# Reordering the output stage of a hybrid decoder layer: recurrent products earlier, transposes later, loads in another order

## The chip, the core and the metric

The kernel runs on one core of a Trainium2 chip. Its engines work side by side, each through its own queue in order: TensorE (PE: matrix products and transposes), VectorE (DVE), ScalarE (ACT), GpSimd (POOL), and SyncE (SP), from whose queue all loads and stores of this stage are issued. They wait for each other through semaphores. PE writes its results to PSUM, here in banks of 128 x 512 float32; the other data lie in SBUF. The metric is the device time of one execution in microseconds (us).

## The reference

One layer of a Hymba-like decoder: 1024 tokens and 16 meta tokens, width 1024, float32. Two groups of heads (a gated delta rule, "GDN", and a forgetting attention, "FoX") share one input projection and one output projection; then comes a SwiGLU block.

```python
u = rmsnorm(h, attn_norm_w[l])
proj = u @ w_in[l]
...
o_gdn = gated_deltanet_group(...)
o_fox = forgetting_attention_group(fq, fk, fv, ff, fgate_b[l]).astype(h.dtype)
h = h + jnp.concatenate([o_gdn, o_fox], axis=-1) @ w_out[l]
h = h + swiglu(rmsnorm(h, ffn_norm_w[l]), w_gate[l], w_up[l], w_down[l])
...
h = rmsnorm(h, final_norm_w)
return h[:, N_META:]
```

The change lies in the next to last product: the output projection, the residual add, the norm ahead of the SwiGLU block, and the transposes that this block needs.

## The kernel before

**Products.** A float32 product is made of three products of parts: each operand is split into a high part (ACT casts, L160) and the rest (DVE subtracts, L161). `mm3` issues high x high (L190), high x low weight (L191), low x high (L192), so the third product of a group is the first that needs the low part of the data. Products are 128 x 128 by 128 x 512; four k-tiles make a group of 12.

**The output stage.** The 1024 rows are 8 tiles of 128, worked in `ORDER` = 0, 4, 1, 5, 2, 6, 3, 7. Below, name(t) is the step of tile t. The left 512 columns of a tile's result are half 0, the right 512 half 1. The steps of a tile:

- `prep_load`: `of` is loaded (512 KB, two attention parts of 128 x 512 each), POOL adds the two parts (L1114), ACT copies the reciprocal row sums into the free half (L1115). There are two `of` buffers.
- `prep_pe`: PE transposes the sums (4 transposes, `rbt`, L1125), DVE multiplies (L1126), ACT and DVE split the result into `ohl`.
- `load_h`: the residual `hst` is loaded (512 KB; for the tiles of `fused` its halves come from `x` and from `h_d`, 256 KB each). There are two `hst` buffers.
- `fox_g`: for the tiles of `fused` (4, 5, 2, 6, 3, 7) the 12 products of the GDN heads for half 1 (`wx<-whi_wo,uh_p`). They depend on nothing of this stage. They are the recurrent products of the title. Their bank (tag "mm", one buffer) is held until `hst` of this tile takes half 1.
- `out_fox(t, 0)`: 12 products (`wof`) and DVE's add to `hst` (L1158). `out_fox(t, 1)`: 12 products (`wx<-wf,ohl` into the bank of `fox_g`, or `wof<-wf`) and the add; then the norm: ACT squares (L1051), DVE scales (`st_f`, L205), POOL takes the power (`st_f`, L206), DVE multiplies by `nwb`, the norm's weights (`xn`, L1053). The tile is stored to `h_d`.
- `u_blocks`: 8 transposes of `xn` into two banks (`u2t`, L1229; tag "tp", three buffers) and their evictions: for tiles 0 to 3 casts and copies on ACT and two subtractions `ul_p` on DVE (L1235); for tiles 4 to 7 also sums for the 7-product scheme of the SwiGLU block, on DVE (`br`, `ub`, `ut`, `ul_p`), ACT and POOL (`br`, L1254, and two `ul_p`).

In step i of the loop (L1402) PE's order is as written: `out_fox(t, 0)`, `prep_pe` of the next tile, `fox_g(t)`, `u_blocks` of the tile before, `out_fox(t, 1)`; for i = 1 and 2 `u_blocks` comes last. What stands ahead of the loop (L1170 to L1192) is the front: the first loads, the last products of the GDN half 0 (`wog`), `rbt`(0), `fox_g`(4), `out_fox`(0, 0), `rbt`(4), `out_fox`(0, 1). The order on DVE, ACT and POOL is set by a scheduler out of this program and the buffers. `issue_after` holds an instruction's place in the queue behind another one. After the loop the first products of the SwiGLU block start (`ga`, `ua`, `gb`, L1324); DVE prepares their weights in the same stretch (`ws_g`, `w_g_p`, `raw_g` and others).

Of the kernel before, what the change touches and what calls it, by code (L numbers as in the profile page):

```python
# [15 lines left out]
P = 128  # L16
# [5 lines left out]
NT = S // P  # L22
# [16 lines left out]
ORDER = (0, 4, 1, 5, 2, 6, 3, 7)  # L39
# [56 lines left out]
def tile_hymba_layer(ctx, tc, x, meta, attn_norm_w, w_in, conv_w, a_log, dt_bias, gdn_norm_w,  # L96
                     fgate_b, w_out, ffn_norm_w, w_gate, w_up, w_down, final_norm_w, out):
    nc = tc.nc
# [8 lines left out]
    def bank(tag, bufs, name):  # L107
        return ps.tile([P, 512], F32, tag=tag, bufs=bufs, name=name)
# [78 lines left out]
    def mm3(dst, pairs, first=True, last=True):  # L187
        n = len(pairs)
        for i, (lh, ll, rh, rl) in enumerate(pairs):
            nc.tensor.matmul(dst, lh, rh, start=(first and i == 0), stop=False)  # L190
            nc.tensor.matmul(dst, lh, rl, start=False, stop=False)  # L191
            nc.tensor.matmul(dst, ll, rh, start=False, stop=(last and i == n - 1))  # L192
# [477 lines left out]
    last = [None]  # L670
# [434 lines left out]
    turn, ofs, ofl, pre_u = {}, {}, {}, {}  # L1105
# [33 lines left out]

    accs, last_h = {}, [None]  # L1140

    def fox_g(tt):
        if tt in fused:
            accs[tt] = bank("mm", 1, f"wx_{tt}")
            mm3(accs[tt], gdn_pairs(tt, 1), last=False)

    def pf_tile(i, nm, dt=F32R):
        return pfp.tile([P, D], dt, tag=f"pf{i}", name=nm)
# [21 lines left out]
    prep_load(ORDER[0])  # L1170
    with tc.issue_after(last_o[0].ins):
        prep_load(ORDER[1])
    with tc.issue_after(ofl[ORDER[1]].ins):
        nc.sync.dma_start(nwb2, ffn_norm_w[0].partition_broadcast(P))
    pfp = woc.enter_context(tc.tile_pool(name="pf", bufs=1, side="right", reuse_waits="tile"))
    wfs = [wout_block(4, 0)]
    rot[0] = 1
    for _ in wout_gdn(1, 1):
        pass
    first_o = prep_pe(ORDER[0])  # L1180
    with tc.issue_after(first_o[0].ins), tc.issue_after(first_o[1].ins):
        wfs.append(wout_block(4, 1, lambda i: [pf_tile(2 * i + c, f"wf{c}_{i}") for c in range(2)]))
    with tc.issue_after(ofl[ORDER[1]].ins):
        load_h(ORDER[0])
    fox_g(ORDER[1])
    prep_load(ORDER[2])
    out_fox(ORDER[0], 0)
    prep_pe(ORDER[1])
    with tc.issue_after(ofl[ORDER[1]].ins):
        load_h(ORDER[1])  # L1190
    out_fox(ORDER[0], 1)
    prep_load(ORDER[3])  # L1192
    peo.close()
# [76 lines left out]
    def w_raw(t, v, f):  # L1270
        return nc.sync.dma_start(t.rearrange("p (k c) -> p k c", k=KT), v[:, :, P * f:P * f + P])
# [129 lines left out]
    with tc.manual_schedule(engines={mybir.EngineType.PE}):  # L1401
        for i, tt in enumerate(ORDER):  # L1402
            if not i:
                continue
            out_fox(tt, 0)
            if i < NT - 1:
                prep_pe(ORDER[i + 1])
                load_h(ORDER[i + 1])
                if 3 < i + 2 < NT:
                    prep_load(ORDER[i + 2])  # L1410
            if i > 2:
                fox_g(tt)
                u_blocks(ORDER[i - 1])
            out_fox(tt, 1)
            if i < 3:
                u_blocks(ORDER[i - 1])
            if i == 2:
                for m, v in (("g", w_g_v), ("u", w_u_v)):
                    raw0[m] = wraw.tile([P, WMAX], F32, tag="raw", name=f"raw_{m}")[:, :D]
                    w_raw(raw0[m], v, 0)  # L1420
            if i == 3:
                with tc.issue_after(tail[0][0].ins):
                    nc.scalar.activation(wo2.tile([P, 1], F32, name="sil"), mhalf[:, 0:1], AF.Silu)
            if i == NT - 1:
# [177 lines left out]
```

## Time and profile before

| | |
|---|---|
| median of 3 runs | 1340.49 us (1338.54 to 1341.32) |
| the profiled execution's own time | 1338.71 us |
| its span in the profile | 1336.7 us |
| granted PE clock, mean of the span | 0.993 |
| PE / DVE / ACT / POOL busy | 97% / 64% / 42% / 32% |
| output stage, `rbt`(0) to the second `gb` product | 620.53 to 711.34 us |

A row of the timeline reads: start, duration, engine, line, operation, output <- inputs, shapes, count; in brackets the idle time of the engine ahead of it and what ended it. Several back-to-back products overlap: a product of 0.39 us starts 0.23 us after the one ahead of it. A row of the chain has the start, the duration and what was worked on; "DMA" there is a transfer from its issue to its landing. A window's row has its length, then the busy time of each engine with its count of instructions, the granted clock, the DMA engines' share and the rate in GB/s.

### The profile page before, as it was taken

To read this page: it belongs to the slowest core of one execution; us is meant where nothing else is said; L and a number is where in the kernel's file an instruction comes from. 1 tells how busy PE (TensorE), PEld (TensorE's weight loads), DVE (VectorE), ACT (ScalarE), POOL (GpSimd) and SP (SyncE) were. 2 spreads that over 40 slices of the span, in tenths; PEclk is the share of its full clock that TensorE was granted. 3 is DMA by queue.
4 is the path that set the end of the run, shared out by engine and by line. 5 is a ranking of instruction groups with operands and counts; after the bars stand their busy time and mean duration, and the time that the engine had idled before them with its cause. 6 is when DMAs were issued, how large, how long until landed. Compare 5 with 4: busy or idle time off the path is not lost.

```text
span 1336.7 us, 20231 instructions
## 1 busy us (share of the span) xinstructions
PE 1299.9 (97%) x7442; PEld 1134.7 (85%) x7442; DVE 849.8 (64%) x1503; ACT 558.5 (42%) x930; POOL 429.7 (32%) x414
## 2 busy tenths in 40 slices
PE   7999999999999999998999999999999999999997
PEld 7999998889999977886777888888888888888886
DVE  5565587847526668895777665665666565355645
ACT  6453454422323367885553233333233343333332
POOL 2110034221012156671431655543344453010301
PEclk8999999899999999999999999999999999999999
DMA  7122536586569598765643654344545547954523
GB/s 249 58 64 64 142 118 180 152 235 182 162 230 321 166 298 228 221 151 156 202 161 112 205 181 148 138 159 155 170 146 172 181 169 258 408 195 177 211 69 126
DMA packets 192954, 237.93 MB, mean 178 GB/s; under 512 B 18896, under 2 KB 144712, under 8 KB 189144
## 3 DMA queue, kind: packets, MB, share of 16 engines
q1 hardware_dynamic: 192856, 236.65, 55.4%
q8 instruction: 58, 0.95, 0.3%
q14 instruction: 40, 0.33, 0.1%
HBM read 159.00 MB, written 77.60 MB: 177 GB/s over the span
## 4 chain that ended last, share of the span: by engine, by line
PE 83%; DMA 6%; DVE 4%; POOL 2%; issue 2%; ACT 1%; SPq 1%; POOLq 0%; DVEq 0%; ACTq 0%
PE xp L1487 8%; PE yp L1487 7%; PE gb L1324 4%; PE ud L1324 4%; PE gd L1324 4%; PE ub L1324 4%; PE ua L1324 4%; PE ga L1324 4%; PE pj_fk L200 4%; PE pj_fq L200 3%; PE ue L1324 2%; PE ge L1324 2%; PE pt L973 2%; PE fv L200 1%; PE pq L473 1%
## 5 line engine op out<-in xcount | busy, mean ns | idle before, releaser
L161 DVE TENSOR_TENSOR al_p<-ra_p,ah_p 128x2048 fp32r<-128x2048 f32 (+1 forms) x21 | 46.6, 2221 | 93.9 <-ACT ah_p L160 93.9
L926 POOL TENSOR_TENSOR bi<-ccol,cr 128x144 f32<-128x144 f32 (+7 forms) x60 | 69.7, 1167 | 51.6 <-DVE sm L942 36.0
L160 ACT CAST ah_p<-ra_p 128x2048 fp32r<-128x2048 f32 (+1 forms) x21 | 37.1, 1766 | 105.7 <-PE xp L1487 48.5
L1487 PE MATMUL xp<-wh_p,ah_p 128*128 128x512 f32 (+1 forms) x187 | 70.5, 377 | 0.7 <-DVE hs L1514 0.7
L1487 PE MATMUL xp<-wl_p,ah_p 128*128 128x512 f32 (+1 forms) x187 | 70.4, 376 | 0.0
L1487 PE MATMUL xp<-wh_p,al_p 128*128 128x512 f32 (+1 forms) x187 | 70.4, 376 | 0.0
L1377 POOL TENSOR_TENSOR gzw<-gzw,uzt 128x512 f32<-128x512 f32 x11 | 18.4, 1673 | 153.7 <-DVE uzt L1368 127.8
L1377 POOL TENSOR_TENSOR gxy<-gxy,uxy 128x512 f32<-128x512 f32 x22 | 39.0, 1771 | 66.9 <-DVE uxy L1368 55.4
L1324 PE MATMUL gb<-uh_p,w_g_p 128*128 128x512 f32 x176 | 57.8, 389 | 0.0
L1324 PE MATMUL ub<-uh_p,w_u_p 128*128 128x512 f32 x176 | 57.7, 389 | 0.0
L1324 PE MATMUL gd<-uh_p,w_g_p 128*128 128x512 f32 x176 | 57.7, 389 | 0.0
L1324 PE MATMUL ud<-uh_p,w_u_p 128*128 128x512 f32 x176 | 57.7, 389 | 0.0
L161 DVE TENSOR_TENSOR w_u_p<-raw_u,w_u_p 128x512 fp32r<-128x512 f32 x42 | 43.0, 1024 | 21.6 <-ACT w_u_p L160 21.4
L161 DVE TENSOR_TENSOR pl<-pt,ph 128x512 fp32r<-128x512 f32 (+1 forms) x96 | 51.8, 552 | 4.3 <-ACT ph L160 3.7
L947 ACT ACTIVATE pr<-pr,sm 128x144 f32<-128x144 f32 (+3 forms) x64 | 50.5, 789 | 9.5 <-DVE sm L942 8.4
L160 ACT CAST ph<-pt 128x512 fp32r<-128x512 f32 (+1 forms) x96 | 45.2, 472 | 18.4 <-PE pt L973 17.8
L1324 PE MATMUL ga<-uh_p,w_g_p 128*128 128x512 f32 x160 | 52.5, 389 | 0.0
L1324 PE MATMUL ua<-uh_p,w_u_p 128*128 128x512 f32 x160 | 52.5, 389 | 0.0
L1487 PE MATMUL yp<-wh_p,ah_p 128*128 128x512 f32 x132 | 51.3, 389 | 0.0
L1487 PE MATMUL yp<-wl_p,ah_p 128*128 128x512 f32 x132 | 51.3, 389 | 0.0
L1487 PE MATMUL yp<-wh_p,al_p 128*128 128x512 f32 x132 | 51.3, 389 | 0.0
L161 DVE TENSOR_TENSOR wl_p<-rw_p,wh_p 128x2048 fp32r<-128x2048 f32 (+1 forms) x21 | 46.9, 2235 | 3.4 <-ACT wh_p L160 3.4
(629 smaller groups left out, 4297.0 us busy)
## 6 DMA issues: line engine op xcount, KB each, us to landing
ra_p<-ao_p SPq DMA_DIRECT2D x14, 1024.0 KB
raw_g<-in_w_gate_dram SPq DMA_DIRECT2D x22, 512.0 KB
raw_u<-in_w_up_dram SPq DMA_DIRECT2D x22, 512.0 KB
raw_d<-in_w_down_dram SPq DMA_DIRECT2D x22, 512.0 KB
wt_p<-raw_d SPq DMA_DIRECT2D x33, 256.0 KB
rw_p<-wt_p SPq DMA_DIRECT2D x8, 1024.0 KB
kk<-k_d SPq DMA_DIRECT2D x14, 520.0 KB
rw_p<-in_w_down_dram SPq DMA_DIRECT2D x6, 1024.0 KB
```

What stands on the lines that cost most here:

```text
L160: cast = nc.scalar.copy(dst_hi, src)
L161: tail[0] = (cast, nc.vector.tensor_sub(dst_lo, src, dst_hi.bitcast(F32)))
L200: nc.tensor.matmul(dst, a, b, start=first, stop=last)
L473: nc.tensor.matmul(pq[:, 256 * i:256 * i + 256], kq[:, 0, c:c + P], kq[:, :, c:c + P], start=True, stop=True)
L926: nc.gpsimd.tensor_tensor(bi[:, :n], ccol[:, h, j:j + 1].broadcast_to([P, n]), cr[:, :n], op=ALU.subtract)
L947: nc.scalar.activation(pr[:, :n], pr[:, :n], AF.Exp, bias=sm[:, np_ - 1:np_], scale=-1.0, accum_out=rsum[:, h, j:j + 1])
L973: nc.tensor.transpose(pt[:rows_k, P * j:P * j + P], pts[j][0][:, c0:c0 + rows_k], ident)
L1324: nc.tensor.matmul(dst, a[:, c], b[:, k], start=(first and k == 0 and i == 0), stop=(k == 3 and i == 2), skip_group_check=not first)
L1377: last_mul[0] = G.tensor_tensor(gs[d], gs[d], us[d], op=ALU.mult)
L1487: nc.tensor.matmul(dst[:, n_], a[:, f, c], b[:, f, n_], start=(first and i == 0 and n == 0), stop=(i == NF - 1 and n == 2), skip_group_che ...
```

## The change

No instruction's work changes. Six edits:

1. `fox_g`(4) is cut in two: 6 of its 12 products come ahead of `rbt`(0), 6 behind.
2. All 12 products of `fox_g`(5) move from the loop to the front, behind `fox_g`(4). Their bank is one of the three of `u2t` (`tag=ps_t`), held until `hst`(5) takes half 1.
3. The load of `nwb` goes from behind the load of `of`(4) to behind those of `hst`(4), so behind the one of `hst`(0) too.
4. `u_blocks` of the tile before comes behind `out_fox(t, 1)` for i = 3 to 6 (of tiles 1, 5, 2, 6) as it did for i = 1 and 2. For i = 7 it stays ahead.
5. The loads of the first SwiGLU weights (`raw_g`, `raw_u`) go behind the load of `of`(5).
6. In the loop `fox_g(t)` runs for i > 3, as tile 5's is done.

```diff
--- before.py
+++ after.py
@@ -1139,10 +1139,11 @@
 
     accs, last_h = {}, [None]
 
-    def fox_g(tt):
+    def fox_g(tt, ks=slice(0, 4), tag=None):
         if tt in fused:
-            accs[tt] = bank("mm", 1, f"wx_{tt}")
-            mm3(accs[tt], gdn_pairs(tt, 1), last=False)
+            if not ks.start:
+                accs[tt] = tag(f"wx_{tt}") if tag else bank("mm", 1, f"wx_{tt}")
+            mm3(accs[tt], gdn_pairs(tt, 1)[ks], first=not ks.start, last=False)
 
     def pf_tile(i, nm, dt=F32R):
         return pfp.tile([P, D], dt, tag=f"pf{i}", name=nm)
@@ -1170,24 +1171,25 @@
     prep_load(ORDER[0])
     with tc.issue_after(last_o[0].ins):
         prep_load(ORDER[1])
-    with tc.issue_after(ofl[ORDER[1]].ins):
-        nc.sync.dma_start(nwb2, ffn_norm_w[0].partition_broadcast(P))
     pfp = woc.enter_context(tc.tile_pool(name="pf", bufs=1, side="right", reuse_waits="tile"))
     wfs = [wout_block(4, 0)]
     rot[0] = 1
     for _ in wout_gdn(1, 1):
         pass
+    fox_g(ORDER[1], slice(0, 2))
     first_o = prep_pe(ORDER[0])
     with tc.issue_after(first_o[0].ins), tc.issue_after(first_o[1].ins):
         wfs.append(wout_block(4, 1, lambda i: [pf_tile(2 * i + c, f"wf{c}_{i}") for c in range(2)]))
     with tc.issue_after(ofl[ORDER[1]].ins):
         load_h(ORDER[0])
-    fox_g(ORDER[1])
+    fox_g(ORDER[1], slice(2, 4))
+    fox_g(ORDER[3], tag=ps_t)
     prep_load(ORDER[2])
     out_fox(ORDER[0], 0)
     prep_pe(ORDER[1])
     with tc.issue_after(ofl[ORDER[1]].ins):
         load_h(ORDER[1])
+        nc.sync.dma_start(nwb2, ffn_norm_w[0].partition_broadcast(P))
     out_fox(ORDER[0], 1)
     prep_load(ORDER[3])
     peo.close()
@@ -1408,16 +1410,18 @@
                 load_h(ORDER[i + 1])
                 if 3 < i + 2 < NT:
                     prep_load(ORDER[i + 2])
-            if i > 2:
+            if i > 3:
                 fox_g(tt)
+            if i == NT - 1:
                 u_blocks(ORDER[i - 1])
             out_fox(tt, 1)
-            if i < 3:
+            if i < NT - 1:
                 u_blocks(ORDER[i - 1])
             if i == 2:
                 for m, v in (("g", w_g_v), ("u", w_u_v)):
                     raw0[m] = wraw.tile([P, WMAX], F32, tag="raw", name=f"raw_{m}")[:, :D]
-                    w_raw(raw0[m], v, 0)
+                    with tc.issue_after(ofl[ORDER[3]].ins):
+                        w_raw(raw0[m], v, 0)
             if i == 3:
                 with tc.issue_after(tail[0][0].ins):
                     nc.scalar.activation(wo2.tile([P, 1], F32, name="sil"), mhalf[:, 0:1], AF.Silu)
```

On PE, at the front: the last `wog` product, `rbt`(0) and the products of tile 4 behind it (`wx_7501`), as they stood before.

```order
L200 MATMUL wog_1_7463<-whi_wo_11_5994,ul_p_4132 128x512
L1125 MATMUL rbt_7479<-ident,of_7437 128x128 x4
L190 MATMUL wx_7501<-whi_wo_10_5988,uh_p_4131 128x512
L191 MATMUL wx_7501<-wlo_wo_10_5989,uh_p_4131 128x512
L192 MATMUL wx_7501<-whi_wo_10_5988,ul_p_4133 128x512
```

The same place in the change, where tile 4's products are `wx_7477`:

```order
L190 MATMUL wx_7477<-whi_wo_10_5988,uh_p_4131 128x512
L191 MATMUL wx_7477<-wlo_wo_10_5989,uh_p_4131 128x512
L192 MATMUL wx_7477<-whi_wo_10_5988,ul_p_4133 128x512
L1125 MATMUL rbt_7485<-ident,of_7437 128x128 x4
L190 MATMUL wx_7477<-whi_wo_11_5994,uh_p_4131 128x512
L191 MATMUL wx_7477<-wlo_wo_11_5995,uh_p_4131 128x512
L192 MATMUL wx_7477<-whi_wo_11_5994,ul_p_4133 128x512
```

The transposes now stand in the middle of tile 4's 12 products; behind the second six come the 12 of tile 5 (`wx_7513`), and only then `wof`(0, 0).

On SP, the loads from `of`(4) (`of_7441`) on, before: `hst_7499` is tile 0's residual, `hst_7541` tile 4's, `of_7514` is tile 1's and `of_7565` tile 5's.

```order
L1113 DMA of_7441<-o_d 128x1024
L1174 DMA nwb_7436<-in_ffn_norm_w_dram 128x1024
L1083 DMA h_d<-ht_1_7461 128x512
L1137 DMA hst_7499<-h_d 128x1024
L1134 DMA hst_7541<-in_x_dram 128x512
L1135 DMA hst_7541<-h_d 128x512
L1113 DMA of_7514<-o_d 128x1024
L1271 DMA raw_g<-in_w_gate_dram 128x8x128
L1271 DMA raw_u<-in_w_up_dram 128x8x128
L1113 DMA of_7565<-o_d 128x1024
L1162 DMA h_d<-hst_7499 128x1024
L1137 DMA hst_7645<-h_d 128x1024
```

And in the change, from the row behind `of`(4) on (tile 0's residual is `hst_7505`, tile 4's `hst_7553`; `of_7526` is tile 1's, `of_7578` tile 5's, `hst_7658` tile 1's residual):

```order
L1083 DMA h_d<-ht_1_7460 128x512
L1137 DMA hst_7505<-h_d 128x1024
L1134 DMA hst_7553<-in_x_dram 128x512
L1135 DMA hst_7553<-h_d 128x512
L1192 DMA nwb_7436<-in_ffn_norm_w_dram 128x1024
L1113 DMA of_7526<-o_d 128x1024
L1113 DMA of_7578<-o_d 128x1024
L1273 DMA raw_g<-in_w_gate_dram 128x8x128
L1273 DMA raw_u<-in_w_up_dram 128x8x128
L1163 DMA h_d<-hst_7505 128x1024
L1163 DMA h_d<-hst_7553 128x1024
L1137 DMA hst_7658<-h_d 128x1024
```

`nwb` went behind four smaller loads and stores, the two weights behind `of`(5), and tile 1's residual behind tile 4's store.

On DVE, in the middle of the stage, from the residual add of tile 5 (`hst_7707<-wof`) on, before: `of_7710` and `ohl_7780` are tile 2's, `xn_1` is tile 1's norm, the `ul_p` are of tile 4.

```order
L1158 TENSOR_TENSOR hst_7707<-wof_0_7766,hst_7707 128x512
L1235 TENSOR_TENSOR ul_p_7613<-ub_7745,uh_p_7612 128x4x128
L1126 TENSOR_TENSOR of_7710<-rbt_7781,of_7710 128x512
L1053 SCALAR_TENSOR_TENSOR xn_1_7728<-hst_7645,st_f_7729,nwb_7436 128x1024
L1235 TENSOR_TENSOR ul_p_7619<-u2t_1_7740,uh_p_7618 128x4x128
L1235 TENSOR_TENSOR ul_p_7617<-ut_7746,uh_p_7616 128x4x128
L161 TENSOR_TENSOR ohl_7780<-of_7710,ohl_7780 128x512
```

And in the change (`hst_7720` is tile 5's, `of_7723` and `ohl_7793` tile 2's):

```order
L1159 TENSOR_TENSOR hst_7720<-wof_0_7779,hst_7720 128x512
L1126 TENSOR_TENSOR of_7723<-rbt_7794,of_7723 128x512
L1053 SCALAR_TENSOR_TENSOR xn_1_7741<-hst_7658,st_f_7742,nwb_7436 128x1024
L1237 TENSOR_TENSOR ul_p_7626<-ub_7758,uh_p_7625 128x4x128
L1237 TENSOR_TENSOR ul_p_7632<-u2t_1_7753,uh_p_7631 128x4x128
L1237 TENSOR_TENSOR ul_p_7630<-ut_7759,uh_p_7629 128x4x128
L161 TENSOR_TENSOR ohl_7793<-of_7723,ohl_7793 128x512
```

`xn`(1) now stands one `ul_p` further ahead; `ohl`(2) is still behind all three `ul_p`. The second of these, `ul_p<-u2t_1`, is the last reader of the bank that the second half of `u2t`(1) gets.

## The prediction

> **What bounds the kernel now.** I read the page first: the totals, then the chain that ended last.
>
> ```profile
> span 1336.7 us, 20231 instructions
> PE 1299.9 (97%) x7442; PEld 1134.7 (85%) x7442; DVE 849.8 (64%) x1503; ACT 558.5 (42%) x930; POOL 429.7 (32%) x414
> PE 83%; DMA 6%; DVE 4%; POOL 2%; issue 2%; ACT 1%; SPq 1%; POOLq 0%; DVEq 0%; ACTq 0%
> ```
>
> TensorE (PE) is busy for 97% of the span and carries 83% of the chain. The change adds and removes no instruction; it only reorders the output stage. So it can earn no more than PE's waits there. These are PE's waits from 616 to 712 us (total, times, longest, in us), then the busy times of that stretch by stage (length, PE, PEld, DVE, ACT, POOL, clock, DMA share, GB/s).
>
> ```profile
> PE u2t L1229 <- DVE xn L1053: 2.9, 4, 1.6
> PE rbt L1125 <- ACT of L1115: 2.1, 2, 1.3
> PE wof L190 <- ACT ohl L160: 0.9, 1, 0.9
> PE gb L1324 <- DVE ul_p L1235: 0.8, 1, 0.8
> ...
> 616.00:636.00 20.00, 16.99 (x79) 12.78 (x79) 7.95 (x13) 6.84 (x11) 4.42 (x4) 1.00 0.81 245
> 636.00:657.00 21.00, 20.45 (x106) 16.56 (x105) 16.59 (x24) 12.20 (x23) 9.87 (x8) 1.00 0.64 216
> 657.00:685.00 28.00, 25.86 (x128) 20.83 (x127) 18.04 (x28) 13.97 (x26) 9.72 (x9) 1.00 0.46 151
> 685.00:711.00 26.00, 25.31 (x122) 20.27 (x119) 24.09 (x37) 17.25 (x32) 9.24 (x7) 1.00 0.42 142
> ```
>
> The waits sum to 2.9 + 2.1 + 0.9 + 0.8 = 6.7 us, 0.5% of the span: the ceiling. The granted clock is 1.00 in every stage, so it decides nothing. The front (616 to 636) is short of data, with DMA at 0.81. The tail (685 to 711) is VectorE's (DVE): 24.09 of its 26 us are busy, on other work than what the change moves on PE. A microsecond won ahead of the tail is kept only if DVE's tail also starts earlier.
>
> **Front: three waits are filled.** The timeline of PE there, and two rows that give the price of a product group:
>
> ```profile
> 619.35 0.39 PE L200 MATMUL wog<-whi_wo,ul_p 128*128 128x512 f32 x1
> 620.53 0.66 PE L1125 MATMUL rbt<-ident,of 128*128 128x128 f32 x4 [0.79 <-ACT of L1115]
> ...
> 628.02 0.66 PE L1125 MATMUL rbt<-ident,of 128*128 128x128 f32 x4 [1.28 <-ACT of L1115]
> ...
> 632.39 0.50 PE L190 MATMUL wof<-whi_wo,ohl 128*128 128x512 f32 x1 [0.94 <-ACT ohl L160]
> ...
> 635.53 0.60 PE L1125 MATMUL rbt<-ident,of 128*128 128x128 f32 x4
> ...
> 640.26 0.50 PE L192 MATMUL wof<-whi_wo,ohl 128*128 128x512 f32 x1
> ...
> 657.08 0.39 PE L190 MATMUL wof<-whi_wo,ohl 128*128 128x512 f32 x1
> ...
> 659.84 0.60 PE L1125 MATMUL rbt<-ident,of 128*128 128x128 f32 x4
> ```
>
> Twelve products take 659.84 - 657.08 = 2.76 us, 0.23 each. Six of wx(4) ahead of rbt(0) cost 1.4 us where PE waited 0.79. The last product of wog starts at 619.35, so rbt(0) starts near 619.35 + 7 x 0.23 = 620.96, 0.43 later than before and without a wait. Then 18 products stand ahead of wof(0,0) instead of 12. With 0.36 for the transposes, 4.14 for the products and 2.76 for wof(0,0), rbt(4) comes near 628.3, where its data were ready at 628.02. The 2.76 us of wx(5) have thus replaced the waits of 0.79 and 1.28 and their restarts.
>
> The third wait, 0.94 us ahead of wof(4,0), hangs on DVE, which stands still for the residual of tile 0 with the product of tile 4 queued behind it. Rows of DVE's timeline, of the chain, of the DMA queue (SPq), of the loads' sizes and of GpSimd's (POOL) timeline:
>
> ```profile
> 630.40 0.69 DVE L1158 TENSOR_TENSOR hst<-wof,hst 128x512 f32<-128x512 f32 x1 [4.43 <-DMA hst<-h_d]
> 623.25 7.06 DMA hst<-h_d
> 625.21 0.49 SPq L1113 DMA_DIRECT2D of<-o_d  x1
> nwb<-in_ffn_norm_w_dram SPq DMA_DIRECT2D x1, 512.0 KB
> 633.12 1.29 POOL L1114 TENSOR_TENSOR of<-of 128x512 f32<-128x512 f32 x1 [5.81 <-DMA of<-o_d]
> ...
> 637.77 1.29 POOL L1114 TENSOR_TENSOR of<-of 128x512 f32<-128x512 f32 x1 [2.10 <-DMA of<-o_d]
> ```
>
> hst(0) takes 7.06 us from issue to landing, with of(4), the broadcast nwb and the write of ht ahead of it. At the stage's 245 GB/s the 0.52 MB of nwb are 2.1 us. So hst(0) lands between 0 and 2.1 us earlier; I take 1.3, a little over the middle, so near 629.1. DVE adds and multiplies and ACT casts (0.69 + 0.69 + 0.62), and ohl(4) is ready near 631.1, ahead of PE's 631.5. Anything from 0.9 on gives the same, since PE isn't there before; at 0 the wait of 0.94 stays.
>
> of(1) gains nothing: the same bytes are ahead of it, nwb only in another place. It lands at 633.1 as before, POOL adds (1.29) and ACT copies (0.6), so rbt(1) starts near 635.1 although PE is there by 634.3. ACT has xn(0) behind that copy, which shifts xn(0) on DVE to about 636.9 to 638.2 and the low half of ohl(1) to 640.1. So the third product of wof(1,0) starts near 640.3, against 640.26, with 2.76 us of wx(5) already done. **Credit at that point: 2.7 us.** The of(5) load goes ahead of the weights and lands up to 2 us before 637.77; nothing waits for it. The load of hst(1) goes behind the store of tile 4:
>
> ```profile
> 638.94 0.32 SPq L1137 DMA_DIRECT2D hst<-h_d  x1
> ```
>
> That store waits for DVE's second add of tile 4, near 639.4, so hst(1) is issued some 0.6 us later. It is first read behind wof(1,0), near 643; I take 0, with +0.6 as the bound.
>
> **Middle: the credit is spent.** Between rbt(2) and u2t(1), wx(5) no longer fills 2.76 us. There the timelines of PE, DVE and POOL show:
>
> ```profile
> 653.41 1.06 PE L1229 MATMUL u2t<-ident,xn 128*128 128x128 f32 x8 [0.51 <-DVE xn L1053]
> 651.98 1.27 DVE L1053 SCALAR_TENSOR_TENSOR xn<-hst,st_f,nwb 128x1024 f32<-128x1024 f32 x1
> 653.18 0.68 DVE L1235 TENSOR_TENSOR ul_p<-u2t,uh_p 128x512 fp32r<-128x512 f32 x1
> 653.78 1.17 DVE L1235 TENSOR_TENSOR ul_p<-ut,uh_p 128x512 fp32r<-128x512 f32 x1
> 655.60 1.06 DVE L161 TENSOR_TENSOR ohl<-of,ohl 128x512 fp32r<-128x512 f32 x1 [0.65 <-ACT ohl L160]
> 652.23 2.17 POOL L1114 TENSOR_TENSOR of<-of 128x512 f32<-128x512 f32 x1 [2.06 <-ACT uh_p L1234]
> 654.36 3.45 POOL L1235 TENSOR_TENSOR ul_p<-br,uh_p 128x512 fp32r<-128x512 f32 x2
> ```
>
> wof(2,0) started at 657.08 on PE, and its low half of ohl(2) was ready at 655.60 + 1.06 = 656.66. So before, DVE had only 0.4 us to spare. DVE must still do xn(1), three ul_p and ohl(2) in a row; the new order puts xn(1) one ul_p earlier (0.68 us) and leaves ohl(2) last. u2t(1) can start near 652.8, but its second half takes the third bank that the held wx(5) took away. It waits for ul_p of u2t_1(4), which now ends near 654.2 behind xn(1). Then wof(2,0) waits for ohl(2), ready near 656.7 to 657.3. I put its third product at 657.5, the time it had before (657.08 + 2 x 0.23): **the 2.7 us are given back.** Bounds: if DVE's row ran without its long pieces (1.17 and 1.06 where 0.68 is normal) and the bank came free at once, 654.5, so 3.0 us kept; if POOL holds DVE up once more, 658.6.
>
> Those long pieces come in pairs: of took 2.17 us on POOL instead of 1.29, beside xn; ul_p took 1.17 instead of 0.68, beside of and ul_p. [...]
>
> **Behind it: two waits covered, one tile later.**
>
> ```profile
> 663.77 1.06 PE L1229 MATMUL u2t<-ident,xn 128*128 128x128 f32 x8 [0.54 <-DVE xn L1053]
> 675.20 1.06 PE L1229 MATMUL u2t<-ident,xn 128*128 128x128 f32 x8 [1.60 <-DVE xn L1053]
> 684.86 1.03 PE L1229 MATMUL u2t<-ident,xn 128*128 128x128 f32 x8
> ```
>
> u2t(5) and u2t(2) move behind 12 more products, whose 2.76 us cover 0.54 and 1.60, with the restarts (the products ahead end 0.70 and 1.77 us before the transposes start) 2.45 us. But u2t(6) itself moves behind 12 products: 684.86 - 2.45 + 2.76 = 685.2 us. DVE's evictions of tile 6, with which its full stretch begins, start 0.3 us later; PE alone runs 2.45 us ahead.
>
> **Tail.** The chain there, and DVE's last wait:
>
> ```profile
> 697.96 0.69 DVE L1158 TENSOR_TENSOR hst<-wx,hst 128x512 f32<-128x512 f32 x1 [1.01 <-PE wx L192]
> ...
> 698.56 0.68 DVE ws_g L1298
> 709.61 1.69 DVE ul_p L1235
> 711.34 2.80 PE gb L1324 x11
> ```
>
> From 698.56 to 711.34 the chain is DVE. The only idle time that it can give up is the 1.01 us at 697.96, which ends with PE; PE is early there now. Of it I take half, 0.5, since POOL's two ul_p of tile 6 can fall beside xn(3). Sum: front -2.7, middle +2.7, behind it +0.3, tail -0.5: **-0.2 us**. The profiled execution took 1338.71 us, so 1338.5; it lies 1.8 under the median of the runs (1340.49), and on the median's footing the time is 1340.3.
>
> **Rivals.** About 0.2%, 2.7 us, is what a measurement of this kernel tells from no change: below 1337.8 or above 1343.2 on the median's footing.
>
> (A) **The credit is kept.** DVE and POOL alternate without the long pieces, and the bank comes free in time. Then u2t(6) starts near 685.2 - 3.0 = 682.2, DVE's stretch begins 2.7 us earlier, and with the 1.01 us at 697.96 the gain is up to 3.7, with part of the last 0.81 us (gb) 4.1: 1336.4. For it: DVE is busy 16.59 of 21 us in the middle. Against it: 655.60 + 1.06 against 657.08.
>
> (B) **POOL takes the turn from DVE.** of(5) is now ready before xn(0) and can start beside it; the two ul_p of tile 6 stand ready beside xn(3). One of(5) of 1.29 us ahead of xn(0) puts the middle at 658.6, +1.1; one ul_p (3.45 / 2 = 1.7) ahead of xn(3) makes u2t(3), and with it DVE's last stretch, 1.7 later. Together 1.1 + 1.7 = 2.8: 1343.3, slower. It decides if POOL's row starts at any moment before xn's, as 652.23 (behind 651.98) just failed to. [...]
>
> (C) **The loads don't do what the reordering says.** hst(0) lands no earlier, the 0.94 us stays and the credit is 1.8. As the middle waits for DVE, nothing more is lost: 1340.3 as well, up to 1341.2 if the middle shifts with it.
>
> **Chances.** Forecast with (C) 0.60; (A) in full or for the most part 0.24; (B) 0.16. The range goes from (A)'s 1336.4 less 0.6 for the spread of runs to (B)'s 1343.3: 1335.8 to 1343.3. Faster by over 0.2%: 0.25 (A and the lower end of the forecast); slower: 0.15; within: 0.60.
>
> **What would show it.** Front: rbt(0), rbt(4) and wof(4,0) without waits, and rbt(1) with one of about 0.7 on ACT's copy. Middle: a new wait of u2t(1) or wof(2,0) on DVE, together 2 to 3 us; if they have none, (A). Behind: u2t(5) and u2t(2) without waits. Tail: gb near 711.3. If xn(0), xn(1) or xn(3) starts behind a POOL row, (B). The forecast is wrong if u2t(6) starts under 683.5 or over 686.5, or if DVE's tail shrinks for another reason.

## The result: 0.14% slower

The changed kernel took 1342.43 us in the median of 20 runs (1340.25 to 1343.90), the kernel before 1340.28 us in 20 runs beside them (1337.53 to 1342.06). The ratio is 1.0014, 95% interval 1.0008 to 1.0020: 2.15 us slower by the medians, where 0.2 us faster was forecast. By the prediction's bound of 0.2% this is still no change, but the sign is clear: the interval lies above 1.

Executions differ by some 5 us in when the output stage begins (its last `wog` product starts at 618.1 to 623.4 us in the profiles of this study). So the stage is measured here from that start; call **S** the time from it to the second `gb` product. Below are the totals of the profile after, then PE's waits from 612 to 716 us and the four stretches that were shown of before (length, PE, PEld, DVE, ACT, POOL, clock, DMA share, GB/s).

```profile
span 1339.1 us, 20231 instructions
PE 1299.9 (97%) x7442; PEld 1133.6 (85%) x7442; DVE 855.6 (64%) x1503; ACT 558.6 (42%) x930; POOL 430.9 (32%) x414
...
PE u2t L1231 <- DVE xn L1053: 3.3, 4, 1.1
PE u2t L1231 <- DVE ul_p L1237: 1.7, 1, 1.7
PE ga L1326 <- DVE ul_p L1237: 1.1, 1, 1.1
PE wof L192 <- DVE ohl L161: 1.0, 2, 0.5
PE gb L1326 <- DVE ul_p L1237: 0.8, 1, 0.8
PE rbt L1125 <- ACT of L1115: 0.5, 1, 0.5
PE wof L190 <- ACT ohl L160: 0.2, 1, 0.2
...
616.00:636.00 20.00, 19.51 (x91) 15.49 (x90) 8.15 (x12) 6.35 (x10) 4.73 (x5) 1.00 0.69 231
636.00:657.00 21.00, 17.44 (x88) 13.15 (x86) 18.68 (x23) 13.34 (x24) 9.80 (x8) 0.99 0.62 215
657.00:685.00 28.00, 27.38 (x127) 22.26 (x128) 20.57 (x29) 12.70 (x23) 9.40 (x8) 0.95 0.47 150
685.00:711.00 26.00, 22.93 (x111) 18.27 (x110) 22.78 (x35) 15.21 (x28) 8.22 (x6) 1.00 0.36 122
```

PE's work is the same to 0.1 us, but DVE's busy time rose from 849.8 to 855.6 us with the same 1503 instructions: some take longer. PE waits 8.6 us in the stage instead of 6.7. The front is full now (19.51 of 20 us busy, 16.99 before), and the waits lie in the second stretch and in the tail. The third stretch has a granted clock of 0.95.

The landmarks of PE, DVE and POOL, in order of time:

```profile
618.10 0.39 PE L200 MATMUL wog<-whi_wo,ul_p 128*128 128x512 f32 x1
627.97 0.69 DVE L1159 TENSOR_TENSOR hst<-wof,hst 128x512 f32<-128x512 f32 x1 [2.87 <-DMA hst<-h_d]
633.88 0.66 PE L1125 MATMUL rbt<-ident,of 128*128 128x128 f32 x4 [0.49 <-ACT of L1115]
635.67 1.29 POOL L1114 TENSOR_TENSOR of<-of 128x512 f32<-128x512 f32 x1
635.74 2.31 DVE L1053 SCALAR_TENSOR_TENSOR xn<-hst,st_f,nwb 128x1024 f32<-128x1024 f32 x1
640.07 0.50 PE L192 MATMUL wof<-whi_wo,ohl 128*128 128x512 f32 x1
650.72 2.40 DVE L1053 SCALAR_TENSOR_TENSOR xn<-hst,st_f,nwb 128x1024 f32<-128x1024 f32 x1
652.29 0.39 PE L192 MATMUL wx<-wf,ohl 128*128 128x512 f32 x1
653.05 1.76 DVE L1237 TENSOR_TENSOR ul_p<-ub,uh_p 128x512 fp32r<-128x512 f32 x1
653.27 0.63 PE L1231 MATMUL u2t<-ident,xn 128*128 128x128 f32 x4 [0.59 <-DVE xn L1053]
655.55 0.63 PE L1231 MATMUL u2t<-ident,xn 128*128 128x128 f32 x4 [1.66 <-DVE ul_p L1237]
655.93 0.49 PE L190 MATMUL wof<-whi_wo,ohl 128*128 128x512 f32 x1
657.13 0.79 PE L192 MATMUL wof<-whi_wo,ohl 128*128 128x512 f32 x1 [0.47 <-DVE ohl L161]
660.83 0.60 PE L1125 MATMUL rbt<-ident,of 128*128 128x128 f32 x4
669.00 0.14 DVE L205 TENSOR_SCALAR st_f<-st_f 128x1 f32<-128x1 f32 x1
670.21 1.29 POOL L1114 TENSOR_TENSOR of<-of 128x512 f32<-128x512 f32 x1 [7.37 <-DVE ut L1254]
673.17 0.54 POOL L206 TENSOR_TENSOR st_f<-st_f,mhalf 128x1 f32<-128x1 f32 x1
673.74 2.31 DVE L1053 SCALAR_TENSOR_TENSOR xn<-hst,st_f,nwb 128x1024 f32<-128x1024 f32 x1 [1.10 <-POOL st_f L206]
676.58 1.17 DVE L1237 TENSOR_TENSOR ul_p<-ut,uh_p 128x512 fp32r<-128x512 f32 x1
677.67 0.68 DVE L161 TENSOR_TENSOR ohl<-of,ohl 128x512 fp32r<-128x512 f32 x1
678.41 0.50 PE L192 MATMUL wof<-whi_wo,ohl 128*128 128x512 f32 x1 [0.48 <-DVE ohl L161]
686.77 1.03 PE L1231 MATMUL u2t<-ident,xn 128*128 128x128 f32 x8
694.18 1.06 PE L1231 MATMUL u2t<-ident,xn 128*128 128x128 f32 x8 [0.84 <-DVE xn L1053]
699.37 0.50 PE L1326 MATMUL ga<-ul_p,whi_g 128*128 128x512 f32 x1 [1.13 <-DVE ul_p L1237]
706.06 1.06 PE L1231 MATMUL u2t<-ident,xn 128*128 128x128 f32 x8 [1.10 <-DVE xn L1053]
713.74 0.50 PE L1326 MATMUL gb<-ul_p,w_g_p 128*128 128x512 f32 x1 [0.81 <-DVE ul_p L1237]
```

Divide the stage at u2t(6), where DVE's full stretch begins. It started 684.86 - 619.35 = 65.51 us into the stage before and starts 686.77 - 618.10 = 68.67 us into it now: +3.16. Ahead of it PE has 12 more products (+2.76), waits 4.7 instead of 5.7 us (-1.0), and works for a while at half its clock (the products from 657.13 to 660.83 take 3.70 us; the same piece took 2.31 before: +1.4). Behind it PE has 12 products less (-2.76) and waits 0.84 + 1.13 + 1.10 + 0.81 = 3.9 instead of 0.22 + 0.81 = 1.0 (+2.9), with +0.4 left for the restarts behind them: the stretch takes 26.97 us instead of 26.48. S is 95.64 instead of 91.99.

### The profile page after: what moved, and what is told of

The parts are those of the page before. It is cut to its first block, busy times and chain, and to the rows that moved or that the text cites. A ratio compares the mean times of both kernels' runs of the same rounds, so it can differ in the third digit from the quotient of the medians.

```text
span 1339.1 us, 20231 instructions
## 1 busy us (share of the span) xinstructions
PE 1299.9 (97%) x7442; PEld 1133.6 (85%) x7442; DVE 855.6 (64%) x1503; ACT 558.6 (42%) x930; POOL 430.9 (32%) x414
## 4 chain that ended last, share of the span: by engine, by line
PE 81%; DMA 6%; DVE 5%; issue 3%; POOL 2%; SPq 1%; ACT 1%; POOLq 0%; DVEq 0%; ACTq 0%
PE xp L1491 8%; PE yp L1491 7%; PE gb L1326 4%; PE ud L1326 4%; PE ub L1326 4%; PE gd L1326 4%; PE ua L1326 4%; PE ga L1326 4%; PE pj_fk L200 4%; PE pj_fq L200 2%; PE ue L1326 2%; PE ge L1326 2%; PE pt L973 2%; PE fv L200 1%; PE pq L473 1%
```

## The experiments

Each row: where u2t(6) starts in the stage, S, the stretch between, and the time as a ratio to the kernel before on the same chip with its 95% interval (6 to 12 runs, 20 of the change). u2t(6), S and the stretch come from one profiled execution each, in us.

| kernel | u2t(6) | S | behind u2t(6) | ratio |
|---|---|---|---|---|
| before | 65.51 | 91.99 | 26.48 | |
| r_before_again | 66.87 | 93.35 | 26.48 | 1.0004 (0.9992 to 1.0015) |
| the change | 68.67 | 95.64 | 26.97 | 1.0014 (1.0008 to 1.0020) |
| r_after_again | 68.46 | 95.43 | 26.97 | 1.0013 (1.0000 to 1.0027) |
| e1_raws_first | 66.59 | 93.57 | 26.98 | 1.0001 (0.9988 to 1.0013) |
| e2_wx5_loop | 70.69 | 97.67 | 26.98 | 1.0024 (1.0012 to 1.0036) |
| e5_filler | 68.44 | 95.42 | 26.98 | 1.0018 (1.0008 to 1.0027) |
| e6_u6_early | 64.53 | 91.57 | 27.04 | 0.9993 (0.9980 to 1.0007) |
| e7_raws_u6 | 63.93 | 90.39 | 26.46 | 0.9991 (0.9980 to 1.0001) |
| e8_pool_behind | 67.52 | 94.50 | 26.98 | 1.0022 (1.0013 to 1.0030) |
| e9_gate_u6 | 64.91 | 91.37 | 26.46 | 0.9994 (0.9985 to 1.0003) |
| e10_late_only | 67.22 | 93.69 | 26.47 | 1.0002 (0.9989 to 1.0015) |
| e11_late_all | 68.40 | 95.37 | 26.97 | 1.0037 (1.0023 to 1.0052) |
| e12_front_only | 67.23 | 93.71 | 26.48 | 1.0022 (1.0008 to 1.0035) |
| e13_mix | 69.37 | 95.82 | 26.45 | 1.0014 (1.0002 to 1.0026) |
| e14_defer | 66.29 | 93.26 | 26.97 | 0.9995 (0.9981 to 1.0010) |
| e15_defer_u6 | 62.99 | 91.30 | 28.31 | 0.9995 (0.9985 to 1.0004) |
| e16_defer_gate | 65.93 | 92.94 | 27.01 | 0.9989 (0.9977 to 1.0001) |
| e17_defer_hold | 61.50 | 90.09 | 28.59 | 0.9954 (0.9937 to 0.9971) |
| e18_hold7 | 69.22 | 96.20 | 26.98 | 1.0007 (0.9996 to 1.0019) |

The two kernels once more, for the spread.

> The kernel before, once more, for how far one profiled execution stands for others. If the stage is decided by its order: S lies within 0.5 us of 91.99, u2t(6) starts 65.5 us after the last wog product, and the eight xn take 1.28 us each as before. Rival (which of POOL and DVE starts first is luck in each execution): one or more xn take about 2.3 us, and S is off by 1 us or more.

> The changed kernel once more, for how far its profile stands for others. If the new waits follow from the order: u2t(6) 67.9 to 68.7 us after the last wog product, S 95 to 95.7, waits again at the second half of u2t(1), at wof(2,0) and wof(3,0) on ohl, and at ga; three or more xn over 2 us. Rival (the low clock behind wof(2,0) made that profile long): without it S is under 94.7.

The S of the change repeats to 0.2 us, with the low clock and three of the four long xn. The kernel before doesn't: S was 93.35 this time, and one xn took 2.13 us. The rival was right there: the profile from which the forecast was made was 1.4 us on the short side. By the second profiles the change costs 95.43 - 93.35 = 2.1 us, which is what the medians show.

**Where u2t(6) stands.** e6 puts only u2t(6) back (its edit stands here); e10 and e11 do edit 4 alone on the kernel before, e10 without tile 6 and e11 in full:

```diff
-            if i == NT - 1:
+            if i >= NT - 2:
                 u_blocks(ORDER[i - 1])
             out_fox(tt, 1)
-            if i < NT - 1:
+            if i < NT - 2:
                 u_blocks(ORDER[i - 1])
```

> The change with u2t(6) alone back ahead of the second 12 products of tile 3. Theory 4 (u2t(6) sets where DVE's full stretch starts, and its 12 products of delay come out at the end): u2t(6) starts 2.8 us earlier, 65.9 us after the last wog product and not 68.67, and S falls by 2 to 2.8, to about 93.2. Rival (DVE's tail is long by its turns with POOL or by tile 3's norm, whatever u2t(6) does): S stays within 0.7 of 95.6.

> The kernel before with edit 4 alone, and of it only tiles 1, 5 and 2: their u2t go behind the second 12 products, u2t(6) stays where it was. S of before was 91.99 and 93.35 in two profiles, u2t(6) 65.51 and 66.87 us after the last wog product. If the covered waits (0.51 to 1.49, 0.54 to 0.67, 1.60) count one to one at the end: no wait at these three u2t, u2t(6) at 63 to 64, S 89.5 to 90.5. Rival (the products ohl behind them then wait, as the middle is DVE's): waits of wof on ohl of 1 to 3 us, S 91.5 to 93.

> The kernel before with edit 4 alone, in full, u2t(6) too. Theory 4: u2t(6) 2.7 us later than in e10_late_only, the stretch from it to the end 27.0 us where it is 26.5 in that run, so S 3.2 us more, 92.5 to 94: the three covered waits paid back by the fourth transposes. Rival (PE, 2.7 us ahead behind u2t(6), shortens the tail): S within 1 us of e10_late_only's.

In e6 u2t(6) came 4.1 us earlier and S fell by 4.1, more than expected, in a profile without a stretch at half clock; the time is no longer above before's. e11 shows that edit 4 alone, in full, is slower by 0.37%. e10, without tile 6, is level with before: the waits of u2t(1) and u2t(5) are gone, but u2t(2) waits 2.39 us for xn(2) where it waited 1.60, with 12 products more ahead of it, and this profile has a stretch at half clock. So covering the waits didn't count one to one; the rival for e10 was nearer. For e11 the expected S (92.5 to 94) was missed too, while its stretch behind u2t(6) was 26.97, as expected.

The column of the stretch is the plainest result: with u2t(6) behind the 12 products it is 26.97 or 26.98 us in all nine such profiles, whatever comes ahead; with u2t(6) ahead of them it is 26.45 to 26.48 in seven of eleven, and 27.0 to 28.6 where another wait fell into it. The 12 products that PE no longer has behind u2t(6) come back there as waits.

**The loads, the early products and the clock.**

> The change with edit 5 undone: the loads of the two first SwiGLU weights go ahead of that of of(5) again. S is the stage from the last wog product to the second gb product: 91.99 us before, 95.64 us with the change. Theory 1 (POOL's add of of(5) started 0.07 us ahead of xn(0) on DVE and held it up by 1.03 us): of(5) comes later, xn(0) takes 1.28 us again, and the third product of wof(1,0) starts 20.9 us after the last wog product and not 21.97; S falls by 0 to 1.1 us. Rival (xn(0) is long for the late load of nwb or for another reason): xn(0) stays at 2.3 us and S at 95.6.

```diff
-                    with tc.issue_after(ofl[ORDER[3]].ins):
-                        w_raw(raw0[m], v, 0)
+                    w_raw(raw0[m], v, 0)
```

xn(0) took 1.28 us again, as theory 1 had it, and S fell by 2.1, more than expected. But rbt(5) came at 24.28 us into the stage, against 24.39 in the change: what xn(0) gave, ACT's late cast of ohl(1) (1.21 us of wait) took. So S fell for what came later: two xn took over 1.3 us instead of four, and wof(3,0) didn't wait. Which load made that difference isn't settled.

> The change with edits 2 and 6 undone: the 12 recurrent products of tile 5 are back in the loop, in their own bank. Theory 2 (the bank held for them makes the second half of u2t(1) wait 1.66 us, and PE's clock falls to half behind this wait): neither wait of u2t(1) remains, the granted clock is 1.00 from 656 to 660, PE waits about 1.2 us again ahead of rbt(4), and S falls to 93 to 94.5. Rival (the later transposes or the loads are what costs): S stays at 95.6 or rises, as 2.76 us of cover in the front are gone.

```diff
-    fox_g(ORDER[3], tag=ps_t)
...
-            if i > 3:
+            if i > 2:
                 fox_g(tt)
```

> e7_raws_u6 (S 90.39) without the early products of tile 5: they are back in the loop in their own bank. If the early wx(5) is worth what it fills (2.1 us of waits in the front): S 92 to 92.7, with rbt(4) waiting 2 us. Rival (its credit is spent in the middle anyway, and its bank costs): S within 0.7 of 90.39 or less.

Theory 2 fell in e2 and its rival held: the bank wait is gone, but rbt(4) waits 2.46 us, u2t(2) 2.58, the clock halves twice, and S is 2 us longer than the change's. In e13 the sign is as expected, the size larger: rbt(4) waits 2.12 us, u2t(2) 2.59, and S is 5.4 us longer than e7's, in a profile with 6.8 us at half clock. The early products are worth their place.

> The change with 8 products more between the two halves of u2t(1), into the bank of wof(2,0), which overwrites them. Theory 3 (PE, idle for most of 653 to 656, is granted half its clock for the next 3.4 us, which costs 1.4 us): the clock stays at 1.00 there, the products of wof(2,0) start 0.23 us apart and not 0.43, rbt(6) starts about 41.3 us after the last wog product and not 42.73, and S falls by 0.5 to 1.4. Rival (the low clock comes from elsewhere, or what is won waits for DVE): the clock is 0.5 all the same, or S stays at 95.6.

```diff
...
+            if g and tt == ORDER[2]:
+                acc = wofs[ORDER[4]] = ps_v(f"wof_{ORDER[4]}_0")
+                for _ in range(8):
+                    nc.tensor.matmul(acc, wfs[0][0][0][:, :P], wfs[0][0][0], start=True, stop=True)
             pt = ps_t(f"u2t_{tt}_{g}").rearrange("p (a b) -> p a b", a=4)
```

The clock stayed at 1.00 and rbt(6) came at 41.59 instead of 42.73, so the low clock does follow PE's idle time there: 3.25 us without a product in the change, at most 0.67 in e5. But wof(3,0) then waited 1.39 us for ohl(3) instead of 0.48, and u2t(6) started at 68.44, 0.2 earlier. xn(2) started 1.4 us earlier there, but then three ul_p stood ahead of ohl(3) instead of two, the first of them 1.78 us long. So the 1.4 us of low clock lie in the shadow of DVE.

**The front alone.**

> The change without edits 4 and 5: the front filled, wx(5) early in a bank of u2t, nwb late, but all u2t where they were and the weights ahead of of(5). The prediction's step (the credit of 2.7 us is spent in the middle): third product of wof(2,0) 38 to 39.3 us after the last wog product as in before (38.18), S 92 to 93. Rival (only the later transposes spent it): that product at 35.5 to 36.5, S 89 to 90.5.

The credit is spent in the middle without edit 4 too, and more than that: PE stood idle for 3.86 us ahead of u2t(1), which came 35.83 us into the stage (34.06 before), and then ran at half clock, so that the third product of wof(2,0) came at 41.58 and rbt(6) at 43.88. S, 93.71, lies 0.7 above what was expected. The rival fell, but the credit went in another place than forecast: wx(5) no longer stood ahead of u2t(1), so PE was there at once, while xn(1), which u2t(1) reads, was ready at 35.68; ohl(2) was ready at 39.05, before wof(2,0) began.

**POOL's turns.** Lock in the expectations of e8 and e9 stands for what theory 1 describes: in the change POOL's add began 0.07 us ahead and xn(0) took 2.31 us, in e1 1.28. One small POOL operation that reads xn stands ahead of POOL's big ones:

```diff
...
+        g = G.tensor_tensor(gate, xns[tt][:, 0:1], xns[tt][:, 0:1], op=ALU.add)
+        with tc.issue_after(g.ins):
```

> The change with POOL's big operations held behind DVE's norm: a POOL operation on one column of xn stands ahead of the adds of of(5), of(6), of(3) (behind xn(0), xn(1), xn(5)) and ahead of the two ul_p of tiles 4 and 5 (behind xn(1), xn(2)). Lock theory: no xn of the first six takes over 1.3 us where the change had 2.31, 2.40, 2.28 and 2.31; u2t(6) starts 1 to 2.5 us earlier than 68.67, and S is 93 to 94.7. Rival (the long xn lie in the shadow of other waits, or POOL's delay costs as much): xn are short, but S stays within 0.7 of 95.6.

The xn of DVE in e8, by its timeline (0, 4, 1, 5 and 2):

```profile
636.99 1.28 DVE L1053 SCALAR_TENSOR_TENSOR xn<-hst,st_f,nwb 128x1024 f32<-128x1024 f32 x1
643.10 1.28 DVE L1053 SCALAR_TENSOR_TENSOR xn<-hst,st_f,nwb 128x1024 f32<-128x1024 f32 x1
652.10 1.28 DVE L1053 SCALAR_TENSOR_TENSOR xn<-hst,st_f,nwb 128x1024 f32<-128x1024 f32 x1
661.56 1.27 DVE L1053 SCALAR_TENSOR_TENSOR xn<-hst,st_f,nwb 128x1024 f32<-128x1024 f32 x1
673.13 1.28 DVE L1053 SCALAR_TENSOR_TENSOR xn<-hst,st_f,nwb 128x1024 f32<-128x1024 f32 x1
```

None is long, where the change had 2.31, 1.27, 2.40, 2.28 and 2.31. So the extra microsecond is POOL's operation beside it, shown by taking it away. u2t(6) came 1.15 us earlier, at the low end of what was expected; the time did not improve (1.0022). wof(2,0) waits 1.93 us for ohl(2) even so. That POOL's later work costs what the short xn give is likely, but not shown.

> The change with edit 5 undone and u2t(6) ahead of the second 12 products of tile 3, e1 and e6 together. If what comes ahead of u2t(6) counts one to one and the two savings (2.1 and 4.1 us of S) are mostly apart: u2t(6) 63.0 to 64.5 us after the last wog product, S 89.5 to 91, some 1.5 us less than before. Rival (both won the same wait): S 91.5 as in e6.

> e7 and e8 together: loads of the weights ahead of of(5), u2t(6) early, POOL held behind xn(0), xn(1), xn(5) and xn(2). If locks, the load order and u2t(6) are the whole cost: S 88 to 90, 2 to 4 us less than before. Rival (POOL's later adds make the transposes rbt wait): rbt waits on ACT's copy by over 1 us, and S is no better than e7's.

e7 does as expected; its time is 0.09% below before's, at the edge of what the runs tell (the interval reaches 1.0001). e9 missed its range: holding POOL back on top gains nothing, though rbt waits only 0.53 us. So POOL's turns with xn are at most a part of the loss.

**DVE's order.** In e14 two of DVE's three ul_p of tile 4 (and of tile 5), and with them POOL's two, are issued behind ohl(2) (and ohl(3)):

```diff
...
+                with tc.issue_after(tail[0][1].ins):
+                    while late and i in (3, 5):
+                        late.pop(0)()
```

> The change with two ul_p of tile 4 (and of tile 5) on DVE held behind ohl(2) (and ohl(3)); POOL's two behind them as before. The prediction's step for the middle (ohl(2) is last of a row of xn(1) and three ul_p on DVE, and so the credit is spent): third product of wof(2,0) 36 to 37.8 us after the last wog product instead of 39.03, no second wait at u2t(1) or one under 0.8, no wait of wof(3,0) on ohl(3), u2t(6) at 65.5 to 66.7, S 92.5 to 93.7. Rival (turns with POOL or the load of of(2) set ohl(2), not its place in the row): that product at 38.5 or later and S at 95 or more.

The middle is free: neither u2t(1) nor wof(2,0) waits, the third product of wof(2,0) comes at 36.10 us and rbt(6) at 38.40 instead of 42.73. Together with e8, where short xn alone didn't free wof(2,0), this shows that DVE's row ahead of ohl(2) spent the credit, as the prediction said. But then u2t(2) waits 2.22 us for xn(2). POOL's timeline in e14 shows why:

```profile
671.35 1.30 POOL L1114 TENSOR_TENSOR of<-of 128x512 f32<-128x512 f32 x1 [8.29 <-DMA of<-o_d]
672.60 1.29 POOL L1257 TENSOR_TENSOR br<-br,ub 128x512 f32<-128x512 f32 x1
673.85 0.55 POOL L206 TENSOR_TENSOR st_f<-st_f,mhalf 128x1 f32<-128x1 f32 x1
```

DVE had its st_f(2) done by 667.2, but on POOL's queue the add of of(7) waits for its load, and st_f(2) stands behind it. In the change it is the same: 669.00 on DVE, 673.17 on POOL. Its chain has the load ahead of the add:

```profile
666.04 4.00 DMA of<-o_d
670.21 1.28 POOL of L1114
```

The load landed at 670.04; the add's row in the timeline names `ut`, which DVE had done at 670.07.

> The change with one POOL operation moved: its add of of(7) stands behind st_f(2) and br of tile 5, not ahead of them. Queue theory (in the change DVE has st_f(2) done at 669.00 and POOL does it at 673.17, as the add ahead of it waits for the load of of(7)): POOL does st_f(2) some 2.5 us earlier, xn(2) starts at 53.5 us after the last wog product or earlier instead of 55.4 to 55.6, wof(3,0) no longer waits for ohl(3), u2t(6) at 67.4 to 67.9 instead of 68.5 to 68.7, S 94.2 to 94.9. Rival (xn(2) waits for its place in DVE's row or for POOL's turn): xn(2) at 55 or later and S 95.3 or more.

```diff
...
+        with tc.issue_after(last_pow[0].ins) if tt == 7 else nullcontext():
             G.tensor_tensor(of[:, 0:4], of[:, 0:4], of[:, 4:8], op=ALU.add)
```

With only that add moved, wof(3,0) no longer waits for ohl(3), and POOL does st_f(2) 1.5 us behind DVE's, not 4.2. But xn(2) itself still started 56.55 us into the stage, behind a ul_p of 1.60 us, and S is 96.20: by what was written down the rival held. The half clock lasted longer in this profile (6.8 us), so it doesn't settle the queue theory, which is borne out for that wait alone; the time (1.0007) can't be told from before's or from the change's.

> e7_raws_u6 (S 90.39) with the same hold. If the middle is DVE's order and u2t(6) counts one to one: third product of wof(2,0) at 36 to 37.5 instead of about 39, S 87.5 to 89, the time 0.1% or more below before's. Rival as above: S 90 or more.

> e15_defer_u6 with POOL's adds of of(6) and of(3) behind xn(1) and xn(5) and its ul_p of tiles 4 and 5 behind xn(1) and xn(2). If the turns with POOL still cost when ohl has its place: no xn over 1.3 us, S 0.5 to 1.5 below e15_defer_u6's. Rival (a short xn only moves the turn to ohl, which POOL's ul_p then holds up): S within 0.5 of e15_defer_u6's or more.

> e15_defer_u6 with the same hold of of(7), and with POOL's two ul_p of tile 6 behind st_f(3). In e15_defer_u6 u2t(2) waited 1.84 us for xn(2) and u2t(3) 1.69 us for xn(3), both with st_f late on POOL. If POOL's queue is what is left: both waits under 0.3, u2t(6) at 60.7 to 61.5 us after the last wog product, the stretch behind it 26.5, S 87.2 to 88.2, the time 0.2 to 0.35% below before's. Rival (the waits only move on): S 90 or more.

e15 frees the middle (u2t(6) at 62.99) and loses 1.9 us of it in the tail, where u2t(3) waits 1.69 us for xn(3): S missed its range. e16 has no long xn, but rbt(6) waits 2.56 us for POOL's later add, with a stretch at half clock behind it: there holding POOL back costs more than it gives. e17 moves two places in POOL's queue instead: the add of of(7) as in e18, and the two ul_p of tile 6 behind st_f(3) (two of DVE's ul_p of tile 6 go with them).

```diff
...
+            if i == NT - 1:
+                with tc.issue_after(last_pow[0].ins):
+                    late.pop(0)()
```

The waits of its PE for xn:

```profile
PE u2t L1236 <- DVE xn L1055: 2.1, 2, 1.9
...
```

u2t(2)'s wait is gone, since xn(2) is done at 51.55 us where it was done at 55.62 in e15, and u2t(6) came at 61.50, as expected; u2t(3)'s stays (1.87), now because POOL's ul_p runs beside xn(3). S is 90.09, above what was expected, and the time is 0.9954 (0.9937 to 0.9971) of before's, 1334.74 us in 6 runs: clearly faster than before. S explains only 1.9 or 3.3 us (by which profile of before) of the 7.4 between the medians; behind the second gb the profiles of both take 625.3 to 625.4 us, and where the rest comes from is open.

## Why the prediction was wrong

**Front: right but for xn(0).** The three waits are filled; rbt(1) waits 0.49 us for ACT (0.7 forecast). The credit at wof(1,0) was put at 2.7 us and was 1.7: its third product starts 640.07 - 618.10 = 21.97 us into the stage, 20.91 before. xn(0) took 2.31 us, since POOL's add of of(5) had started 0.07 us ahead of it. That is the first half of rival (B), at its price of 1.1.

**Loads: right.** DVE's first add of tile 0 waited until 627.97 instead of 630.40, 1.2 us earlier in the stage (1.3 taken).

**Middle: right in kind, a little short.** u2t(1) waits for xn(1) as before (0.59 us, 0.51 before), and the waits of its second half and of wof(2,0) are new (1.66, 0.47); e14 with e8 shows that DVE's row is what spends the credit. The slack of 0.4 us that I read there was 0.9, as the low half of ohl(2) is first read by the third product, at 657.53 before. The third product of wof(2,0) starts 39.03 us into the stage, against 38.18 forecast: three of DVE's rows were long beside POOL's (2.40, 1.76, 1.15), near the upper bound (658.6, so 39.25).

**Behind it: this is the step that failed.** "u2t(5) and u2t(2) move behind 12 more products, whose 2.76 us cover 0.54 and 1.60." In the change neither waits. But I took xn(2) as fixed, and it is done 57.95 us into the stage where it was done at 55.70 before, so covering the wait for it wins nothing: where PE reaches u2t(2) sooner and xn(2) is late, PE waits there again, 2.39 us in e10, 2.31 in e11, 2.22 in e14. And the evictions move with the transposes. These are rows of DVE in the kernel before:

```profile
670.14 0.68 DVE L1235 TENSOR_TENSOR ul_p<-ut,uh_p 128x512 fp32r<-128x512 f32 x1
...
673.77 1.28 DVE L1053 SCALAR_TENSOR_TENSOR xn<-hst,st_f,nwb 128x1024 f32<-128x1024 f32 x1 [1.53 <-POOL st_f L206]
674.97 0.68 DVE L161 TENSOR_TENSOR ohl<-of,ohl 128x512 fp32r<-128x512 f32 x1
```

There the last ul_p of tile 5 was done ahead of xn(2), and ohl(3) came right behind it. Now xn(2), two ul_p and then ohl(3) stand in a row, just as for ohl(2), and xn(2) comes late for POOL's queue; wof(3,0) waits for ohl(3), which is ready at 678.35. I worked that row out for the middle and not for its repetition one tile pair later. From the third product of wof(2,0) to u2t(6) it takes 29.64 us, where 27.67 were forecast: +2.0. Of these 1.4 are the half clock, which I had put at nothing; e5 takes 29.28 without it, as wof(3,0) then waits 1.39 us.

The row alone isn't the cost. e1 has it too, with three ul_p, and takes 27.61 us, as forecast. There xn(2) starts 671.75 - 619.34 = 52.41 us into the stage and not 55.64:

```profile
671.75 1.63 DVE L1053 SCALAR_TENSOR_TENSOR xn<-hst,st_f,nwb 128x1024 f32<-128x1024 f32 x1
```

The other eight profiles with edit 4 in full have xn(2) at 53.7 to 56.7 us and take 29.28 to 32.51. The kernels with u2t(6) ahead of the 12 products agree, for which the forecast would be 27.67 - 2.76 = 24.91: e7 takes 24.90 with xn(2) at 52.47, e15 27.25 with xn(2) at 53.33, and e17, which is e15 with POOL's queue moved, 24.87 with xn(2) at 50.28. So the step fails where xn(2) is late. That POOL's queue makes it late is shown by e15 against e17; in the order of the change itself e18 leaves it open.

**Tail: wrong in sign.** I gave it 0.5 us, as PE is ahead there. The stretch behind u2t(6) is 26.97 us whatever PE has done ahead: 0.5 longer, not shorter. PE's lead is worth nothing where DVE's full stretch (24.09 of 26 us before) begins with u2t(6). The right sum was: u2t(6) later by x, the end later by x + 0.5.

**The base.** The profile before was 1.4 us shorter than its repetition, by luck in the middle: there the third product of wof(2,0) starts 39.39 us into the stage. That doesn't excuse the sign: 0.85 + 2.0 + 1.0 us against it is more. By the second profiles the change gains 0.95 us up to that product (38.44), loses 2.5 behind it (30.02 against 27.48) and 0.5 in the tail: 2.1 together. So the 0.85 of the middle is within what a repetition moves, and the step behind it fails by either pair.

Rival (B) named the right side and the right mechanism for part of it (the long xn), but not the place that counted: with the first six xn all short (e8) S is still 94.50. No run shows its other term as it was meant, xn(3) held up by a whole row of POOL (1.7 us): xn(3) took 1.27 us in the change, and 2.30 in e17, where a ul_p of POOL had begun 0.56 us ahead of it, so 1.03 more. Rival (A) would have needed DVE's order to change; e14 shows that the credit then survives the middle. Rival (C) fell with the loads.

## What to carry to other kernels

When a step is moved, write out the queue of every engine that works on its output, at each place where the pattern repeats: an eviction that lands between a norm and the next tile's operand can cost as much as the wait that was covered, and a wait for a row that comes later itself isn't won by covering it. Divide the stage where another engine becomes full, and count on each side work and waits apart; here work moved to the near side of that point was lost, and a lead on the far side was worth nothing. And take a second profile of the kernel before when the forecast is smaller than a microsecond or two.

## What the runs showed of the hardware

Long rows come in pairs on DVE and POOL, and of xn and POOL's add of `of` the one that starts a moment earlier keeps its length. In the 11 profiles in which both queues were read (before, the change, r_after_again, e11 to e18), the two meet 21 times. Where the add began first (8 times, by 0.03 to 0.59 us), it took 1.26 to 1.30 us and xn 1.76 to 2.33: POOL's add at 635.67 against xn at 635.74. Where xn began first by 0.24 us or more (12 times), xn took 1.27 to 1.29 us and the add 1.44 to 2.19. Starts as near as 0.02 us don't tell: xn at 650.72 took 2.40 us beside an add of 1.30 that the profile has at 650.74. The extra 1.03 us of xn(0) lie within the 1.22 that POOL's add still ran (635.67 + 1.29 - 635.74), and in e8, which holds that add back, xn(0) took 1.28. One small operation was long too: a st_f took 2.13 us on POOL at 702.46, where the change's other seven took 0.54 to 0.56, while DVE issued one operation behind the other; no run takes these away.

In the output stage PE's granted clock halved for a while at pauses in which PE had no products. The rows of the windows of the change, in the columns as above:

```profile
653.00:656.00 3.00, 1.07 (x9) 0.90 (x9) 3.00 (x4) 1.46 (x4) 2.93 (x2) 1.00 0.50 173
656.00:657.00 1.00, 0.67 (x4) 0.21 (x2) 1.00 (x2) 0.59 (x1) 0.00 (x0) 0.76 0.02 6
657.00:658.00 1.00, 0.87 (x2) 0.77 (x3) 1.00 (x3) 0.29 (x1) 0.00 (x0) 0.50 0.00 0
658.00:659.00 1.00, 1.00 (x3) 0.72 (x3) 0.98 (x3) 1.00 (x3) 0.00 (x0) 0.50 1.15 164
659.00:660.00 1.00, 1.00 (x4) 0.80 (x3) 0.05 (x1) 0.82 (x2) 0.56 (x1) 0.54 0.50 135
660.00:661.00 1.00, 1.00 (x7) 0.77 (x6) 0.00 (x0) 0.00 (x0) 0.00 (x0) 1.00 0.93 361
```

PE ran at 0.50 for 3.4 us (0.24 / 0.5 + 2 + 0.46 / 0.5, from the rows between 656 and 660), with products 0.43 us apart instead of 0.23. Its 1.07 busy us from 653 to 656 were transposes but for the last 0.07: from the end of the product at 652.29 to the one at 655.93 there was none for 3.25 us. Nine of the 20 profiles have such a stretch there, neither of the kernel before; eight stretches lasted 3.4 us and two, in e13 and e18, 6.8. Seven of the ten come with one pause without a product of 3.21 us or more, and no such pause of the stage is without a stretch: four start 0.1 to 0.6 us behind it, three inside it (1.9 us after its start in e2's first, 2.4 in e16, 4.6 in e12). Pauses of 3.03 to 3.13 us (e6, e11, e14) had none. Transposes ran in the seven pauses and didn't keep the clock up. The other three (r_after_again, e8, e18) come with two pauses of 1.4 to 2.2 us with two products between them, a pattern that e1 and e7 have too (2.3 and 1.6 us), without a stretch. In e5 eight products in the pause kept the clock at 1.00. What sets the moment and the length of a stretch isn't shown.
